# Turning activations by VectorE and a DRAM round trip in place of TensorE transposes, in a two-block fp32 model on one core

## The chip, the core and the metric

The kernel runs on one core of one Trainium2 chip, as one program. The metric is the device time of one execution in microseconds (us), the median of several runs. The engines are named as in the profile: PE (TensorE, matmuls; PEld is its weight load), DVE (VectorE), ACT (ScalarE), POOL (GpSimd), SP (SyncE, which here only issues loads).

## The reference, cut to what matters

A sequence of 256 rows of width 1024 runs, in fp32, through two stacks.

```
first block, 4 layers i:
  h = rms_norm(x);  h = mixer_i(h)          # 0: retention, 1: conformer, 2: short conv, 3: retention
  x = x + rms_norm(h)
  h = relu(rms_norm(x) @ w1)^2 @ w2         # MLP, 1024 -> 4096 -> 1024
  x = x + rms_norm(h)
retention: q,k,v,g = x @ w_in (1024 -> 6144); q,k = rotary(q), rotary(k)
           y = chunked retention(q,k,v), normalised a head; out = (silu(g) * y) @ w_out
short conv: gb,gc,h = x @ w_in;  out = (gb * depthwise_conv3(gc * h)) @ w_out
second block, 2 layers:
  FFN (silu(x@w1) * (x@w3)) @ w2 (1024 -> 2816 -> 1024), layer norm
  token mixing (RWKV-7, GLA, gated delta rule), layer norm
  FFN, layer norm; per-layer-embedding gate, layer norm
```

Every large product has the activations as one operand and a weight matrix streamed from DRAM as the other. Weights are about 470 MB in all.

## The kernel before, in words

**Halves and units.** The 256 rows are two halves, h = 0 and 1, of 128 rows. The weights are a list of *units*, one tile of 128 x 1024 each (the `plan_*` functions). `drive` walks through the list, segment by segment; a segment is a mixer, an MLP, an FFN or the like. At step i half 0 gets unit i and half 1 unit i - lag, where `PACE` gives (lag, ahead, load) for each kind of stage: "1" for the first block, "A" for the FFNs, "M" for token mixing, "B" for its branch products, "P" for the last gate. So at the start of a segment half 0 runs `lag` units alone, and at its end half 1 does, while half 0's normalisation and new left operands are made. A unit is used twice, then released.

**Loading and casting.** `fill` loads up to `load` units ahead (SP, L200) into "raw" buffers, of which there are 3 and 2 more in "1" and "A", and splits up to `ahead` units ahead into a high and a low part in fp32r: `split_unit` copies to `wh` on ACT (L222) and makes `wl` = raw - wh on DVE (L223). There are 4 + 4 slots for these pairs in "1" and "A". A load waits for the cast that frees its raw buffer, a cast for the release of a slot by half 1.

**The product.** `mm3` (matmuls are recorded at L59) multiplies a 128 x 128 block of the left operand, split in the same way (t2h, t2l), in three products into each 512-column group of PSUM: high by high, high by low, low by high. In an MLP or FFN product w1 both groups of 512 go to one bank `mm`, two k-blocks a unit.

**Left operands.** A left operand must have the contracted dimension on partitions, so activations, which come out with rows on partitions, are turned. `tr` (its transposes are recorded at L66) makes four 128 x 128 transposes on PE by the identity into a PSUM bank `tp`; `split` (L348 on ACT, L349 on DVE) reads it and makes t2h and t2l.

**MLP** (`mlp`): the order of units is w1(0), then for each group g of 512 hidden columns w1(g+1), w2(g). After w1(g) ACT makes the relu (L459), DVE its square (L461). For group 0 the turn and split follow w1(1); the others are turned at the second unit of the w2 before them. Eight groups of four + four units.

**FFN** (`ffn`): the same with eleven groups of 256 columns, four units f1 and two f2 a group, silu on ACT (L858), the product on DVE (L860), two transposes a group.

**Retention**: q and k are rotated on DVE (L534 to L540) and turned at once, then copied to SBUF by ACT (rT, L543); 16 units later v is complete and the attention products start. The gated output y2 (L593) is turned and split as soon as each is made, before the product with w_out, whose 16 k-blocks read four such blocks in order. **Short convolution**: gc * h is turned, copied into a window by ACT (L759) and convolved on DVE.

**Buffers.** `B2` gives working tiles from two rings: "s2" of 512 columns, "s1" of up to 264; their sizes are in `RINGS`. In an FFN all group tiles are of the ring "s1".

**Order.** Instructions are issued by each engine in order. `issue_after(ins)` keeps what its block records behind `ins` in that engine's queue.

Of the kernel before, what the change touches and what calls it, by code (L numbers as in the profile page):

```python
# [19 lines left out]

PACE = {"1": (4, 2, 8), "A": (4, 2, 8), "M": (0, 4, 6), "B": (4, 1, 6), "P": (6, 1, 8)}

# [4 lines left out]
RM = (42, 20)  # L27
RINGS = {"1": (30, 6), "A": (20, 6), "M": RM}
SIDE_1 = 1.6
# [21 lines left out]
class Builder:  # L51
    def __init__(s, ctx, tc, io):
# [140 lines left out]
    def load_unit(s, i, early):  # L193
        tag = s.take(s.rawq, early)
        if tag is None:
            return False
        s.slot[i] = [tag, None]
        r = s.r[i] = s.tile_of(tag, F32)
        for dst, src in s.plan[i][1]:
            s.nc.sync.dma_start(dst(r), src)  # L200
        return True

    def split_unit(s, i, early):

        nc = s.nc
        r, n = s.r[i], s.width[i]
        if s.plan[i][0] in EXACT:
            s.w[i] = r
            return True
        tag = s.take(s.whq, early)  # L210
        if tag is None:
            return False
        s.slot[i][1] = tag
        wh, wl = s.tile_of(tag, F32R), s.tile_of(tag, F32R, "l")
        with ExitStack() as st:
            if 2 <= i < 10:

                for ins in s.first_split:
                    st.enter_context(s.tc.issue_after(ins))
            if s.hold is not None and s.hold[0] <= i < s.hold[0] + 4:  # L220
                st.enter_context(s.tc.issue_after(s.hold[1]))
            c = nc.scalar.copy(wh[:, 0:n], r[:, 0:n])  # L222
            nc.vector.tensor_tensor(wl[:, 0:n], r[:, 0:n], wh[:, 0:n].bitcast(F32), op=ALU.subtract)  # L223
# [119 lines left out]
    def split(s, src):  # L343
        nc = s.nc
        n = src.shape[1]
        hh = s.B2((128, n, 128), "t2h", F32R)
        ll = s.B2((128, n, 128), "t2l", F32R)
        a = nc.scalar.copy(hh, src)  # L348
        b = nc.vector.tensor_tensor(ll, src, hh.bitcast(F32), op=ALU.subtract)  # L349
        if s.splits < 2:  # L350
            s.first_split = a.ins, b.ins
        s.splits += 1
        return hh, ll

    def tr(s, src, n=4):
# [3 lines left out]
        return tp  # L359

    def tr_split(s, src):
        return s.split(s.tr(src))

    def linear(s, lhs, KT, name, n=1024, out=None):
# [82 lines left out]
    def mlp(s, h, lhs, rin):  # L447
        nc = s.nc
        out = [s.acc(), s.acc()]
        r = {}  # L450

        def w1(g):
            mm = s.mmb()
            for k in range(0, 8, 2):
                W = yield "w1"
                for kk in range(2):
                    s.mm3(lhs, k + kk, W, [(mm, kk * 512, 512, k + kk == 0, k + kk == 7)])
            a = s.B2(name="relu")
            nc.scalar.activation(a, mm, AF.Relu, scale=rin)  # L459
            a2 = s.B2(name="relu2")  # L460
            nc.vector.tensor_tensor(a2, a, a, op=ALU.mult)  # L461
            r[g] = a2

        yield from w1(0)
        for g in range(8):
            if g < 7:
                yield from w1(g + 1)
            at = nxt if g else [s.tr_split(r.pop(g))]
            for k in range(4):
                W = yield "w2"  # L470
                if g < 7 and k == 1:
                    nxt = [s.tr_split(r.pop(g + 1))]
                s.mm3(at, k, W, [(out[c], c * 512, 512, g == 0 and k == 0, g == 7 and k == 3) for c in range(2)])
        return out
# [49 lines left out]
    def rotary(s, h, ps, rin):  # L524
# [3 lines left out]
        out = []  # L528
        for g in range(2):
# [10 lines left out]
            nc.vector.tensor_tensor(r, a, b, op=ALU.add)  # L540
            tp = s.tr(r.rearrange("p h d -> p (h d)"))
            t = s.B2((128, 4, 128), "rT")
            nc.scalar.copy(t, tp)  # L543
            out.append(t)
        return out

    def retention(s, h, lhs, rin, j):
        nc = s.nc
        sh = s.sh
        q = yield from s.linear(lhs, 8, "ret")  # L550
        qT = s.rotary(h, q, rin)
        k = yield from s.linear(lhs, 8, "ret")
        kT = s.rotary(h, k, rin)
        vs = []
        for c in range(2):
            v = yield from s.linear(lhs, 8, "ret")
            for g in range(2):
# [25 lines left out]
        gn = s.layer_vec(("gn", j), s.io["ret_gn_g"][j])  # L583
        yT = []
        for c in range(2):
            g = yield from s.linear(lhs, 8, "ret")
            for d in range(2):
# [155 lines left out]
    def short_conv(s, h, lhs, rin, j):  # L743
        nc, sh = s.nc, s.sh
        us = []
        for c in range(2):
            ps = yield from s.linear(lhs, 8, "sc1")
            a = s.B2(name="sca")
            nc.scalar.mul(a, ps[0], rin)
            p = s.B2(name="scp")  # L750
            nc.vector.scalar_tensor_tensor(p, ps[1], rin, a, op0=ALU.mult, op1=ALU.mult)
            tp = s.tr(p)
            win = s.pool.tile([128, 4, 130], F32, tag="swin", bufs=4, name="swin")
# [4 lines left out]
            sh["sc", c] = win  # L758
            nc.scalar.copy(win[:, :, 2:130], tp)  # L759
            u = s.B2((128, 4, 128), "scu")  # L760
# [6 lines left out]
            us.append(u)  # L767
        ps = yield from s.linear(lhs, 8, "sc_b")
        hT = []
# [76 lines left out]
    def ffn(s, h, lhs):  # L846
# [4 lines left out]
        def w1(g):  # L851
            mm = s.mmb()
            for k in range(0, 8, 2):
                W = yield "f1"
                for kk in range(2):
                    s.mm3(lhs, k + kk, W, [(mm, kk * 512, 512, k + kk == 0, k + kk == 7)])
# [3 lines left out]
            nc.vector.tensor_tensor(b, a, mm[:, 256:512], op=ALU.mult)  # L860
            r[g] = b

        yield from w1(0)
        for g in range(11):
            if g < 10:
                yield from w1(g + 1)
            at = nxt if g else [s.split(s.tr(r.pop(g), 2)[:, 0:2, :])]
            for k in range(2):
                W = yield "f2"
                if g < 10 and k == 1:  # L870
                    nxt = [s.split(s.tr(r.pop(g + 1), 2)[:, 0:2, :])]
                s.mm3(at, k, W, [(out[c], c * 512, 512, g == 0 and k == 0, g == 10 and k == 1) for c in range(2)])
        return out
# [994 lines left out]
```

## Time and profile before

| | |
|---|---|
| median of 3 runs | 3031.95 us (3026.77 to 3034.68) |
| the profiled execution's own time | 3031.14 us |
| its span, first to last instruction | 3029.3 us |
| granted PE clock | 0.994 |
| busy: PE, DVE, ACT, POOL | 2949.2, 1928.9, 1525.4, 216.6 us |
| transposes on PE of relu, glu, rr, y, scp | 256, 176, 72, 64, 16 |

The profile is of one execution. A row of a group of instructions reads: line of the kernel, engine, operation, output<-inputs, shapes, count | busy us, mean ns of one | idle us of the engine just before them, and what ended it. A row of the timeline reads: start, length, line, operation. A row of the DMA view ends with the KB of one transfer and the median us from issue to landing. A row of waits reads: who waited for whom, us in total, times, longest. Matmuls are pipelined, so their lengths overlap; the distance of their starts tells the pace.

### The profile page before, as it was taken

The page shows a single profiled execution, that of the slowest core. Times are in us where ns is not written, and L with a number is a line of the kernel's source. Part 1 is how long each engine was busy: PE and PEld are TensorE (multiplying, and loading weights), DVE is VectorE, ACT ScalarE, POOL GpSimd, SP SyncE. Part 2 cuts the span into 40 slices and gives each one's busy share as a digit, 9 for nine tenths or more (in the row PEclk, how much of TensorE's full clock was granted, in tenths as well). Part 3 has the DMA queues.
Part 4 walks back from the last instruction along what each step waited for, and adds up shares of the span by engine and source line. Part 5 has one row for each costly group of instructions (what it writes and reads, how often), then busy time and mean ns, then how long its engine had stood idle before and what let it go on. Part 6 is the DMA issues. An engine that isn't in the chain of part 4 may idle for free. (4 is left out here: it accounts for less than half of the span.)

```text
span 3029.3 us, 48491 instructions
## 1 busy us (share of the span) xinstructions
PE 2949.2 (97%) x19034; PEld 2368.4 (78%) x19034; DVE 1928.9 (64%) x3039; ACT 1525.4 (50%) x2348; POOL 216.6 (7%) x352
## 2 busy tenths in 40 slices
PE   8999998999999999999999999999999999999998
PEld 6778877787788778787887777778878778777786
DVE  7565578656755766655557857565665576666656
ACT  4454454545544534544447674444454486643543
POOL 0000025000000000200001000000010000000000
PEclk9999999999999999999999999999999999999999
DMA  7556642566666555665655334366666553334763
GB/s 242 155 180 190 185 152 81 176 187 193 179 191 184 184 167 173 211 187 178 187 173 165 93 92 120 118 207 189 188 203 188 147 147 93 106 112 130 223 188 120
DMA packets 256325, 498.52 MB, mean 165 GB/s; under 512 B 24917, under 2 KB 125473, under 8 KB 256096
## 3 DMA queue, kind: packets, MB, share of 16 engines
q1 hardware_dynamic: 247424, 470.82, 51.1%
q0 software_dynamic: 8096, 22.49, 2.5%
q8 instruction: 150, 2.46, 0.3%
q10 hardware_dynamic: 576, 2.10, 0.2%
q14 instruction: 79, 0.65, 0.1%
HBM read 494.28 MB, written 1.05 MB: 164 GB/s over the span
## 5 line engine op out<-in xcount | busy, mean ns | idle before, releaser
L59 PE MATMUL acc<-wh,t2h 128*128 128x512 f32 (+1 forms) x1512 | 622.0, 413 | 8.6 <-ACT t2h L348 6.1
L223 DVE TENSOR_TENSOR whl<-raw,wh 128x1024 fp32r<-128x1024 f32 x341 | 414.7, 1218 | 293.6 <-ACT wh L222 292.1
L59 PE MATMUL acc<-whl,t2h 128*128 128x512 f32 (+1 forms) x1512 | 594.8, 395 | 0.4 <-DVE whl L223 0.4
L222 ACT CAST wh<-raw 128x1024 fp32r<-128x1024 f32 x341 | 356.7, 1046 | 376.3 <-PE acc L59 252.6
L59 PE MATMUL acc<-wh,t2l 128*128 128x512 f32 (+1 forms) x1512 | 511.5, 395 | 2.1 <-DVE t2l L349 2.0
L223 DVE TENSOR_TENSOR whxl<-raw,whx 128x1024 fp32r<-128x1024 f32 x272 | 330.3, 1216 | 228.6 <-ACT whx L222 228.1
L222 ACT CAST whx<-raw 128x1024 fp32r<-128x1024 f32 x272 | 284.0, 1046 | 272.7 <-PE mm L59 133.9
L59 PE MATMUL acc<-whx,t2h 128*128 128x512 f32 (+1 forms) x856 | 347.9, 407 | 3.0 <-ACT t2h L348 2.9
L59 PEld LDWEIGHTS acc<-wh,t2h 128*128 128x128 f32 x1512 | 286.6, 190 | 78.7 <-ACT t2h L348 14.1
L59 PE MATMUL acc<-whxl,t2h 128*128 128x512 f32 (+1 forms) x856 | 336.3, 393 | 3.3 <-DVE whxl L223 3.3
L59 PEld LDWEIGHTS acc<-wh,t2l 128*128 128x128 f32 x1512 | 284.9, 189 | 67.4 <-DVE t2l L349 5.5
L59 PEld LDWEIGHTS acc<-whl,t2h 128*128 128x128 f32 x1512 | 287.0, 190 | 53.1 <-DVE whl L223 2.0
L59 PE MATMUL mm<-whx,t2h 128*128 128x512 f32 x800 | 313.2, 392 | 2.1 <-ACT whx L222 1.7
L59 PE MATMUL mm<-whx,t2l 128*128 128x512 f32 x800 | 312.1, 390 | 0.8 <-DVE t2l L349 0.8
L59 PE MATMUL mm<-whxl,t2h 128*128 128x512 f32 x800 | 311.8, 390 | 0.8 <-DVE whxl L223 0.8
L59 PE MATMUL acc<-whx,t2l 128*128 128x512 f32 (+1 forms) x856 | 283.6, 392 | 0.5 <-DVE t2l L349 0.5
L223 DVE TENSOR_TENSOR whl<-rawx,wh 128x1024 fp32r<-128x1024 f32 x145 | 177.4, 1225 | 140.8 <-ACT wh L222 140.4
L223 DVE TENSOR_TENSOR whxl<-rawx,whx 128x1024 fp32r<-128x1024 f32 x142 | 173.4, 1222 | 124.9 <-ACT whx L222 124.7
L222 ACT CAST wh<-rawx 128x1024 fp32r<-128x1024 f32 x145 | 152.1, 1050 | 151.9 <-PE acc L59 97.2
L222 ACT CAST whx<-rawx 128x1024 fp32r<-128x1024 f32 x142 | 148.5, 1048 | 140.1 <-PE mm L59 94.6
L59 PEld LDWEIGHTS acc<-whx,t2h 128*128 128x128 f32 x856 | 161.1, 188 | 38.8 <-ACT t2h L348 4.5
L59 PEld LDWEIGHTS acc<-whxl,t2h 128*128 128x128 f32 x856 | 161.5, 189 | 35.9 <-DVE whxl L223 4.8
(613 smaller groups left out, 4143.7 us busy)
## 6 DMA issues: line engine op xcount, KB each, us to landing
raw<-in_mlp_w SPq DMA_DIRECT2D x153, 512.0 KB, 3.7
raw<-in_w_in SPq DMA_DIRECT2D x128, 512.0 KB, 3.7
raw<-in_ffn_w SPq DMA_DIRECT2D x216, 256.0 KB, 3.1
rawx<-in_mlp_w SPq DMA_DIRECT2D x103, 512.0 KB, 3.7
rawx<-in_ffn_w SPq DMA_DIRECT2D x136, 256.0 KB, 3.1
raw<-in_ret_w_in SPq DMA_DIRECT2D x58, 512.0 KB, 4.3
raw<-in_ffn_w SPq DMA_DIRECT2D x53, 512.0 KB, 3.7
rawx<-in_ret_w_in SPq DMA_DIRECT2D x38, 512.0 KB, 4.5
```

Of the source, the lines that this page charges most:

```text
L59: r = m0(out, a, b, **k)
L222: c = nc.scalar.copy(wh[:, 0:n], r[:, 0:n])
L223: nc.vector.tensor_tensor(wl[:, 0:n], r[:, 0:n], wh[:, 0:n].bitcast(F32), op=ALU.subtract)
```

## The change

Activations of MLP, FFN, rotary q and k, gated retention output and short convolution are no longer turned by PE, except for the last group of each MLP and FFN. A new function `tr_dma` turns them in three steps: DVE transposes the 32 x 32 blocks inside the tile (into `tz`); POOL stores the result to a DRAM tile `td` (128 rows of 2 KB, or 1 KB for an FFN's 256 columns); SP loads it back into `ty` in four loads of 32 partitions, each with rows of 512 (256) bytes, so that the blocks land in their places. The loads are put behind the newest weight load in SP's queue. The split (or the copies rT and of the window) reads `ty` in SBUF and is put behind the newest weight cast in ACT's and DVE's order.

The split moves: in MLP and FFN to the third unit of the next w1, in the rotary to the fifth unit of v's second part, for the first two blocks of y2 to the fifth unit of g's second part and for the other two to the fifth unit of the product with w_out, in the short convolution to the fifth unit of the next product. `linear` has a hook `mid` for it, called at k = 4.

Beside this the lag of stages "1" and "A" goes from 4 to 5, "B" from lag 4 and 1 ahead to lag 3 and 2 ahead, and the ring "s1" of stage "A" from 6 to 12 tiles.

```diff
-PACE = {"1": (4, 2, 8), "A": (4, 2, 8), "M": (0, 4, 6), "B": (4, 1, 6), "P": (6, 1, 8)}
+PACE = {"1": (5, 2, 8), "A": (5, 2, 8), "M": (0, 4, 6), "B": (3, 2, 6), "P": (6, 1, 8)}
-RINGS = {"1": (30, 6), "A": (20, 6), "M": RM}
+RINGS = {"1": (30, 6), "A": (20, 12), "M": RM}
...
+        s.dram = pool("dram", 4, space=bass.MemoryType.DRAM)
...
-            s.nc.sync.dma_start(dst(r), src)
+            s.last_load = s.nc.sync.dma_start(dst(r), src).ins
...
+        s.last_cast = c.ins
...
+    def tr_dma(s, src, n):
+        nc = s.nc
+        z = s.B2((128, 4, n, 32), "tz")
+        nc.vector.transpose(z, src.rearrange("p (c a j) -> p a c j", a=4, j=32))
+        d = s.dram.tile([128, 4, n * 32], F32, tag=f"td{n}", bufs=4, name="td")
+        nc.gpsimd.dma_start(d, z.rearrange("p a c j -> p a (c j)"))
+        y = s.B2((128, 4, n, 32), "ty")
+        with s.tc.issue_after(s.last_load):
+            for a in range(4):
+                nc.sync.dma_start(y[32 * a:32 * a + 32].rearrange("i b c j -> i b (c j)"),
+                                  d.rearrange("(b i) a x -> a i b x", b=4)[a])
+        return y.rearrange("p b c j -> p c b j")
+
+    def split_late(s, src):
+        with s.tc.issue_after(s.last_cast):
+            return s.split(src)
...
+            if k == 4 and mid:
+                mid()
...
+                if k == 4 and g:
+                    at[g - 1] = [s.split_late(r.pop(g - 1))]
...
-            r[g] = a2
+            r[g] = s.tr_dma(a2, 4) if g < 7 else a2
...
-            at = nxt if g else [s.tr_split(r.pop(g))]
             for k in range(4):
                 W = yield "w2"
-                if g < 7 and k == 1:
-                    nxt = [s.tr_split(r.pop(g + 1))]
+                if g == 6 and k == 1:
+                    at[7] = [s.tr_split(r.pop(7))]
...
-            tp = s.tr(r.rearrange("p h d -> p (h d)"))
-            t = s.B2((128, 4, 128), "rT")
-            nc.scalar.copy(t, tp)
-            out.append(t)
+            out.append(s.tr_dma(r.rearrange("p h d -> p (h d)"), 4))
...
-                yT.append(s.tr_split(y2))
-        out = yield from s.linear(yT, 16, "ret_o")
+                yy.append(s.tr_dma(y2, 4))
+        out = yield from s.linear(yT, 16, "ret_o", mid=late)
...
-            r[g] = b
+            r[g] = s.tr_dma(b, 2) if g < 10 else b
...
-                if g < 10 and k == 1:
-                    nxt = [s.split(s.tr(r.pop(g + 1), 2)[:, 0:2, :])]
+                if g == 9 and k == 1:
+                    at[10] = [s.split(s.tr(r.pop(10), 2)[:, 0:2, :])]
```

More of the change, by code (lines that the diff above doesn't have):

```diff
@@ L347, in split @@
         ll = s.B2((128, n, 128), "t2l", F32R)
[L348 to L349 removed]
+        cut = (lambda t: t.rearrange("p c (b j) -> p c b j", j=32)) if len(src.shape) == 4 else (lambda t: t)
+        a = nc.scalar.copy(cut(hh), src)
+        b = nc.vector.tensor_tensor(cut(ll), src, cut(hh.bitcast(F32)), op=ALU.subtract)
         if s.splits < 2:
@@ L467, in mlp @@
                 yield from w1(g + 1)
-            at = nxt if g else [s.tr_split(r.pop(g))]
             for k in range(4):
                 W = yield "w2"
-                if g < 7 and k == 1:
-                    nxt = [s.tr_split(r.pop(g + 1))]
-                s.mm3(at, k, W, [(out[c], c * 512, 512, g == 0 and k == 0, g == 7 and k == 3) for c in range(2)])
+                if g == 6 and k == 1:
+                    at[7] = [s.tr_split(r.pop(7))]
+                s.mm3(at[g], k, W, [(out[c], c * 512, 512, g == 0 and k == 0, g == 7 and k == 3) for c in range(2)])
         return out
@@ L540, in rotary, with rotated @@
             nc.vector.tensor_tensor(r, a, b, op=ALU.add)
-            tp = s.tr(r.rearrange("p h d -> p (h d)"))
-            t = s.B2((128, 4, 128), "rT")
-            nc.scalar.copy(t, tp)
-            out.append(t)
+            out.append(s.tr_dma(r.rearrange("p h d -> p (h d)"), 4))
+        return out
+    def rotated(s, ys):
+        out = []
+        with s.tc.issue_after(s.last_cast):
+            for y in ys:
+                t = s.B2((128, 4, 128), "rT")
+                s.nc.scalar.copy(t.rearrange("p c (b j) -> p c b j", j=32), y)
+                out.append(t)
         return out
@@ L550, in retention, with turn @@
         q = yield from s.linear(lhs, 8, "ret")
-        qT = s.rotary(h, q, rin)
+        qy = s.rotary(h, q, rin)
         k = yield from s.linear(lhs, 8, "ret")
-        kT = s.rotary(h, k, rin)
-        vs = []
+        ky = s.rotary(h, k, rin)
+        vs, qT, kT = [], [], []
+        def turn():
+            qT.extend(s.rotated(qy))
+            kT.extend(s.rotated(ky))
         for c in range(2):
-            v = yield from s.linear(lhs, 8, "ret")
+            v = yield from s.linear(lhs, 8, "ret", mid=turn if c else None)
             for g in range(2):
@@ L583, in retention @@
         gn = s.layer_vec(("gn", j), s.io["ret_gn_g"][j])
-        yT = []
+        yT, yy = [], []
+        late = lambda: yT.extend(s.split_late(yy.pop(0)) for _ in range(2))
         for c in range(2):
-            g = yield from s.linear(lhs, 8, "ret")
+            g = yield from s.linear(lhs, 8, "ret", mid=late if c else None)
             for d in range(2):
@@ L745, in short_conv, with taps @@
         us = []
[L746 to L752, printed above, removed]
+        def taps(c, y):
             win = s.pool.tile([128, 4, 130], F32, tag="swin", bufs=4, name="swin")
@@ L758, in short_conv @@
             sh["sc", c] = win
-            nc.scalar.copy(win[:, :, 2:130], tp)
+            with s.tc.issue_after(s.last_cast):
+                nc.scalar.copy(win[:, :, 2:130].rearrange("p c (b j) -> p c b j", j=32), y)
             u = s.B2((128, 4, 128), "scu")
@@ L767, in short_conv @@
             us.append(u)
-        ps = yield from s.linear(lhs, 8, "sc_b")
+        ys = []
+        mid = lambda c: lambda: taps(c, ys[c])
+        for c in range(2):
+            ps = yield from s.linear(lhs, 8, "sc1", mid=mid(0) if c else None)
+            a = s.B2(name="sca")
+            nc.scalar.mul(a, ps[0], rin)
+            p = s.B2(name="scp")
+            nc.vector.scalar_tensor_tensor(p, ps[1], rin, a, op0=ALU.mult, op1=ALU.mult)
+            ys.append(s.tr_dma(p, 4))
+        ps = yield from s.linear(lhs, 8, "sc_b", mid=mid(1))
         hT = []
@@ L854, in w1 @@
                 W = yield "f1"
+                if k == 4 and g:
+                    at[g - 1] = [s.split_late(r.pop(g - 1))]
                 for kk in range(2):
@@ L866, in ffn @@
                 yield from w1(g + 1)
-            at = nxt if g else [s.split(s.tr(r.pop(g), 2)[:, 0:2, :])]
             for k in range(2):
                 W = yield "f2"
-                if g < 10 and k == 1:
-                    nxt = [s.split(s.tr(r.pop(g + 1), 2)[:, 0:2, :])]
-                s.mm3(at, k, W, [(out[c], c * 512, 512, g == 0 and k == 0, g == 10 and k == 1) for c in range(2)])
+                if g == 9 and k == 1:
+                    at[10] = [s.split(s.tr(r.pop(10), 2)[:, 0:2, :])]
+                s.mm3(at[g], k, W, [(out[c], c * 512, 512, g == 0 and k == 0, g == 10 and k == 1) for c in range(2)])
         return out
```

4 lines of the change are left out of this document (3 added, 1 removed).

## The prediction

> **What bounds the kernel now.** I read the page's head first, then a table by stage (one MLP, one FFN), then the chain that ended last, then TensorE's timeline around one transpose.
>
> ```profile
> span 3029.3 us, 48491 instructions
> PE 2949.2 (97%) x19034; PEld 2368.4 (78%) x19034; DVE 1928.9 (64%) x3039; ACT 1525.4 (50%) x2348; POOL 216.6 (7%) x352
> q1 hardware_dynamic: 247424, 470.82, 51.1%
> ```
>
> ```profile
> 845.00:1012.00 167.00, 167.00 (x768) 137.91 (x767) 92.92 (x93) 81.56 (x95) 0.55 (x1) 1.00 0.62 186
> 1425.00:1592.00 167.00, 167.00 (x756) 137.24 (x756) 88.52 (x104) 74.43 (x100) 0.00 (x0) 1.00 0.60 182
> ```
>
> ```profile
> 2304.93 8.16 PE mm L59 x36
> ```
>
> The stage rows (length, then PE, PEld, DVE, ACT and POOL busy, granted clock, DMA share, GB/s) are the inside of an MLP and of an FFN. PE is busy for all 167.00 us at clock 1.00, while DVE has 92.92 and 88.52, ACT less, and the DMA engines 0.62 and 0.60. The chain row gives PE's pace: 36 matmuls in 8.16 us, 0.227 us each. So these stages end when PE's stream ends, and an instruction taken out of that stream is time, if nothing else becomes late. A weight unit is twelve such matmuls (two halves, two column groups, three products): 2.72 us, or 1.36 us for one half alone.
>
> **What is removed.** The price of a transpose is how far it pushes the next matmuls apart.
>
> ```profile
> 604.76 0.39 PE L59 MATMUL mm<-whx,t2l 128*128 128x512 f32 x1
> 604.99 0.60 PE L66 MATMUL tp<-ident,relu 128*128 128x128 f32 x4
> 605.35 0.48 PE L59 MATMUL acc<-wh,t2h 128*128 128x512 f32 x1
> 605.66 0.40 PE L59 MATMUL acc<-whl,t2h 128*128 128x512 f32 x1
> 605.90 0.40 PE L59 MATMUL acc<-wh,t2h 128*128 128x512 f32 x1
> ...
> 1477.58 0.39 PE L59 MATMUL mm<-wh,t2l 128*128 128x512 f32 x1
> 1477.81 0.38 PE L66 MATMUL tp<-ident,glu 128*128 128x128 f32 x2
> 1477.95 0.48 PE L59 MATMUL acc<-whx,t2h 128*128 128x512 f32 x1
> 1478.26 0.39 PE L59 MATMUL acc<-whxl,t2h 128*128 128x512 f32 x1
> 1478.49 0.40 PE L59 MATMUL acc<-whx,t2h 128*128 128x512 f32 x1
> ```
>
> ```profile
> L66 PE MATMUL tp<-ident,relu 128*128 128x128 f32 x256 | 38.3, 272 | 0.0
> ```
>
> From 604.76 to 605.90 lie three matmul steps, which undisturbed take 3 x 0.227 = 0.68 us; they took 1.14. Four transposes cost 0.46 us. The same sum for two (1477.58 to 1478.49) gives 0.91 - 0.68 = 0.23 us. The mean of 272 ns in the last row is a pipelined duration and no price: 528 of them by it would be 144 us, by the starts they are 61.
>
> By the code the change takes away: in the MLPs 4 layers x 2 halves x 7 groups = 56 sets of four (224 of the 256 in the row), 56 x 0.46 = 25.8 us; in the FFNs 4 x 2 x 10 = 80 pairs, 80 x 0.23 = 18.4 us; rotary 2 layers x 2 halves x (q, k) x 2 = 16 sets, gated retention output 16, short convolution 4: 36 x 0.46 = 16.6 us. Together 528 transposes, **60.8 us** of PE. The last group of each MLP and FFN stays on PE.
>
> **What is added, and where it hides.** For each of the 172 blocks: one VectorE transpose, one store by POOL, four loads by SP, each of 32 partitions.
>
> ```profile
> L1107 DVE STREAM_TRANSPOSE invTT<-invT 128x256 f32<-128x256 f32 x20 | 8.7, 435 | 0.1
> L1107 DVE STREAM_TRANSPOSE invTT<-invT 128x128 f32<-128x128 f32 x20 | 6.1, 307 | 0.3
> L147 POOL DMA_DIRECT2D v<-in_norm_g x32 | 18.3, 573 | 58.7 <-DVE t L420 43.3 <-DVE xn L427 14.1 <-DVE xn L404 0.9
> ```
>
> ```profile
> 600.72 0.33 SPq L200 DMA_DIRECT2D rawx<-in_mlp_w  x1
> ```
>
> DVE: 128 more columns cost 0.128 us, so 256 take 0.435 and 512 about 0.69 (estimate from the two rows). 92 x 0.69 + 80 x 0.435 = 98 us, all beside PE: in an MLP group (8 units, 21.8 us) two transposes add 1.4 us to a DVE that is 56% busy. POOL: 172 x 0.573 = 99 us on an engine at 7%. SP: 688 issues x 0.33 = 227 us; SP does nothing but issue loads. Splitting then reads SBUF, not PSUM; I give that no price. None of the three comes near PE's 97%.
>
> DMA: the 172 round trips move 69 MB (92 x 512 KB and 80 x 256 KB, store and load together). Priced by bytes like the queue's row (51.1% for 470.82 MB) that is 7.5 points more over the span; priced by packets, with 128 + 512 rows a block, 110,080 packets and 51.1% for 247,424, it is 22.7. By stage: an MLP group of 21.8 us gets 1.05 MB, 0.16 more by bytes and 0.37 by packets, so 0.78 to 0.99; an FFN group of 16.3 us (6 units) gets 0.52 MB, so 0.71 to 1.09. I take the byte end: the two stage rows move almost the same GB/s at the same share though the FFN's f1 weights come in 1 KB rows and the MLP's in 2 and 4 KB rows, so the share follows bytes.
>
> **The latency, and who waits.** The split of the turned block sits in ACT's queue behind the newest weight cast, and the four loads in SP's behind the newest weight load. If the block is not back, ACT stops and the casts behind it wait, then PE.
>
> ```profile
> L459 ACT ACTIVATE relu<-mm,rin 128x512 f32<-128x512 f32 x64 | 44.2, 690 | 70.1 <-PE mm L59 70.1
> L461 DVE TENSOR_TENSOR relu<-relu 128x512 f32<-128x512 f32 x64 | 44.0, 688 | 33.4 <-ACT relu L459 33.4
> L860 DVE TENSOR_TENSOR glu<-silu,mm 128x256 f32<-128x256 f32 x88 | 36.7, 417 | 30.9 <-ACT silu L858 30.9
> L858 ACT ACTIVATE silu<-mm 128x256 f32<-128x256 f32 x88 | 33.8, 384 | 87.0 <-PE mm L59 87.0
> L349 DVE TENSOR_TENSOR t2l<-tp,t2h 128x512 fp32r<-128x512 f32 x144 | 96.9, 686 | 18.9 <-ACT t2h L348 16.1
> L348 ACT CAST t2h<-tp 128x512 fp32r<-128x512 f32 x144 | 83.1, 586 | 86.2 <-PE tp L66 85.3 <-PE acc L59 0.3
> L349 DVE TENSOR_TENSOR t2l<-tp,t2h 128x256 fp32r<-128x256 f32 x88 | 37.0, 420 | 9.7 <-ACT t2h L348 9.7
> L348 ACT CAST t2h<-tp 128x256 fp32r<-128x256 f32 x88 | 32.6, 371 | 29.6 <-PE acc L59 26.3 <-PE tp L66 3.3
> L59 PE MATMUL acc<-wh,t2h 128*128 128x512 f32 (+1 forms) x1512 | 622.0, 413 | 8.6 <-ACT t2h L348 6.1 <-DVE rb L537 1.7 <-ACT sg L590 0.5
> ```
>
> ```profile
> raw<-in_mlp_w SPq DMA_DIRECT2D x153, 512.0 KB, 3.7
> gv<-in_ret_gn_g POOLq DMA_DIRECT2D x8, 256.0 KB, 5.8
> out<-x ACTq DMA_DIRECT2D x2, 512.0 KB, 2.7
> raw<-in_w_in SPq DMA_DIRECT2D x8, 16.0 KB, 3.1
> ```
>
> No POOL store is in the trace. Its bounds are 2.7 us (the only store, on idle engines at the end) and 5.8 us (the slowest POOL load); I take 4.2, between them, as the store runs among weight loads. A small load lands after 3.1 us, and four issues take 1.3. MLP: 0.69 + 0.69 + 0.69 + 2.7 to 5.8 + 1.3 + 3.1 = 9.2 to 12.3 us to a block that is back, then 1.27 to split. FFN: 0.38 + 0.42 + 0.44 and the same = 8.3 to 11.4 us, then 0.79.
>
> The room in the steady state, from the code: in an MLP six units pass before the split (w2's four, two of the next w1), 16.3 us, in an FFN four, 10.9 us. So MLP blocks are back in time, FFN blocks too but for the last 0.5 us of the bound. Rotary, retention output and short convolution have four units or more: hidden as well.
>
> The first group of each of the eight MLP and FFN runs has less. Half 0 needs it five units later, of which the first runs without half 1: 1.36 + 3 x 2.72 = 9.5 us; half 1 has about 12.2. MLP, block and split: 10.5 to 13.6, late by 1.0 to 4.1 and 0 to 1.4. FFN: 9.1 to 12.2, late by 0 to 2.7 and 0. Four of each: 4 to 33 us, less up to 8 us, since PE already idles there (8.6 us in all before the first matmuls of a split). I take **+10**, ends 0 and +25.
>
> **Slots, queues, lag.** With lag 5 and 2 ahead, eight units are alive in eight slots, where one was spare.
>
> ```profile
> L222 ACT CAST wh<-raw 128x1024 fp32r<-128x1024 f32 x341 | 356.7, 1046 | 376.3 <-PE acc L59 252.6
> L223 DVE TENSOR_TENSOR whl<-raw,wh 128x1024 fp32r<-128x1024 f32 x341 | 414.7, 1218 | 293.6 <-ACT wh L222 292.1
> SPq L200 <- DVE whl L223: 1176.7, 383, 39.5
> L66 PE MATMUL tp<-ident,xn 128*128 128x128 f32 x128 | 20.5, 289 | 13.2 <-DVE xn L404 10.1 <-DVE xn L427 3.1
> ```
>
> A cast already waits for PE to free its slot (252.6 us). It then needs 1.05 + 1.22 = 2.27 us and will have two units, 5.4 us, instead of three: 3.2 us of slack for an ACT that is held. I take **+3**, ends 0 and +20. SP already waits 3.1 us a time for a raw buffer (1176.7 / 383); a load is issued about 3.5 units, 9.5 us, before its cast and lands in 3.7, so 5.8 us of delay by a store's landing and four issues stay hidden. Lag 5 gives 1.36 us more of half 1's matmuls over each layer boundary, where PE idles before the transposes of xn for 13.2 us; **-6**, ends 0 and -17 (a dozen boundaries).
>
> Sum on the profiled execution (span 3029.3 us, its own time 3031.1): 3031.1 - 60.8 + 10 + 3 - 6 = 2977.3; the median of the runs, 3031.95, lies 0.8 above it, so **2978**. The ends of the terms make 2953 to 3017.
>
> **Rivals.**
> *Held ACT, slower.* The split waits in ACT's queue, in the FFNs, where the room is least. Past 10.9 us of room and 3.2 of slack, every further microsecond is lost once for each of 80 blocks. It turns the sign at 10.9 + 3.2 + 60.8/80 = 14.9 us. The upper chain of 11.4 plus one mean load wait of 3.1 on SP is 14.5, so a little more does it: at 15.3 us, 80 x 1.2 = 96 lost, 3031.95 - 60.8 + 96 = 3067. Against it: the chain must be 3.5 us above the bound from rows. Chance 0.10.
>
> *DMA engines become the bound, no change.* At the packet end an FFN group needs 1.09 of its 16.3 us: 1.5 x 40 group times = 60 us, giving back the gain: 3031. For it: rows of 256 bytes, smaller than any bulk load here. Chance 0.06.
>
> *POOL's store is held up by DVE.* A store whose issue stretches over two DVE casts (2 x 1.22 us) makes the chain 2.4 us longer. FFN 13.8 is still inside 14.1, so the steady state holds, but the 16 first blocks lose 2.4 each: 38 us on top, 3016. Against it: POOL's issues took 573 ns on average in a program whose DVE is busy 64%. Chance 0.05. The Trainium skill, "SBUF — State Buffer", section "SBUF: two separate sides", warns that DVE operations that use the port pair they share with GpSimd lock it out of writing descriptors, and gives about 620 ns for such a transfer alone and 3100 beside a DVE copy. By that, the delay would be 2.5 us (an estimate from that page); the 573 ns row does not show it.
>
> *More than forecast.* If boundaries close fully and first groups hide, 3031.95 - 60.8 - 17 = 2954. Inside the main case.
>
> **How the numbers follow.** Main case 0.79, whose own range is 2953 to 3017. Beside it the rivals 0.10, 0.06 and 0.05. The range 2950 to 3017 leaves out the slower and the no-change case, 0.16, and a little of the main one. Measurement of this kernel can tell about 0.3%, 9 us. Faster: 0.79 + 0.05 = 0.84; same 0.06; slower 0.10.
>
> **What would show it.** PE's L66 rows should fall by 528, the tp rows of rr, y and scp vanish, PE's busy time drop by some 60 us at the same share; DVE's L1107-like transposes rise by about 98 us. In the waits, ACT's split should wait on DMA only in the first groups. I am wrong if ACT's split waits on the load of the block all through the FFNs, or if casts and then PE wait on weight loads, or if the DMA share in the FFN window passes 0.9.

## The result, and the profile after

The changed kernel takes **3066.99 us** (median of 4 runs, 3059.68 to 3074.29) where the kernel before, timed beside it, takes 3030.31: a ratio of 1.0118 (95% interval 1.0101 to 1.0135), 36.7 us slower. The forecast was 2978. The profiled execution took 3063.9 us.

The page's head and the granted clock, in which before had PE busy for 2949.2 us and a clock of 0.994:

```profile
span 3062.1 us, 49546 instructions
PE 2917.7 (95%) x18506; PEld 2332.7 (76%) x18506; DVE 2014.2 (66%) x3211; ACT 1517.8 (50%) x2348; POOL 308.8 (10%) x524
```

```profile
core 0: 3062.1 us, clock 0.983
```

PE has 528 instructions fewer, but is busy for only 31.5 us less, since it ran slower (the clock), and it idles longer. The groups say before which instruction (columns as before), and the waits say for whom:

```profile
L59 PE MATMUL acc<-wh,t2h 128*128 128x512 f32 (+1 forms) x1512 | 620.8, 411 | 61.5 <-ACT t2h L351 37.1 <-ACT sg L630 16.2 <-DVE rb L565 6.6
L371 POOL DMA_DIRECT2D td<-tz x172 | 93.8, 545 | 1342.8 <-DVE tz L369 1317.6 <-DVE ang L528 13.4 <-issue 7.8
L369 DVE STREAM_TRANSPOSE tz<-relu 128x512 f32<-128x512 f32 x56 | 39.9, 712 | 1.9
L369 DVE STREAM_TRANSPOSE tz<-glu 128x256 f32<-128x256 f32 x80 | 35.6, 445 | 2.5
```

```profile
ACT t2h L351 <- DMA ty<-td: 84.5, 45, 5.8
PE acc L59 <- ACT t2h L351: 41.4, 28, 6.6
PE acc L59 <- ACT sg L630: 16.2, 7, 7.4
```

```profile
SPq L375 <- DMA td<-tz: 414.7, 146, 10.2
```

The idle time before these matmuls went from 8.6 to 61.5 us; 37.1 of it was ended by a split, 16.2 by a silu. ACT's splits waited 45 times for a turned block, while SP stood 146 times before a block's loads until the store had landed: the blocks are late in some places and not in others. The next rows are from a table by stretches (columns as in the prediction's stage rows); the first is the inside of an FFN:

```profile
1470.00:1590.00 120.00, 120.00 (x526) 97.87 (x525) 69.44 (x87) 54.49 (x73) 7.59 (x14) 1.00 0.72 219
```

There PE is busy for all 120.00 us at full clock with the DMA engines at 0.72: this stretch of the steady state loses nothing. Three places that do lose time follow, each from the timeline (start, length, engine, line; in brackets the idle time before and what ended it).

**The first group of an MLP, half 1.** Rows of ACT, DVE, POOL, SP, ACT and PE, in order of time:

```profile
260.44 0.68 ACT L486 ACTIVATE relu<-mm,rin 128x512 f32<-128x512 f32 x1
262.43 0.71 DVE L369 STREAM_TRANSPOSE tz<-relu 128x512 f32<-128x512 f32 x1
263.44 0.54 POOL L371 DMA_DIRECT2D td<-tz  x1 [4.73 <-DVE tz L369]
265.91 0.85 SPq L201 DMA_DIRECT2D raw<-in_mlp_w  x2
266.85 1.81 SPq L375 DMA_DIRECT2D ty<-td  x4
273.54 0.62 ACT L351 CAST t2h<-ty 128x512 fp32r<-128x512 f32 x1 [4.85 <-DMA ty<-td]
274.21 0.50 PE L59 MATMUL acc<-wh,t2h 128*128 128x512 f32 x1 [2.57 <-ACT t2h L351]
```

From the start of the relu to the start of the split lie 13.1 us; the prediction had 9.2 to 12.3. The store's part is as foreseen (3.4 us to the loads). The loads' part is not: 6.7 us from their first issue, where 1.3 + 3.1 = 4.4 had been put. They stand right behind two weight loads of 512 KB each, and by the first of these stretches the DMA engines are full (1.08):

```profile
268.70:273.50 4.80, 2.94 (x13) 2.09 (x12) 1.23 (x1) 0.00 (x0) 0.00 (x0) 1.00 1.08 303
273.50:279.00 5.50, 4.79 (x14) 3.79 (x15) 3.23 (x4) 2.46 (x4) 0.54 (x1) 0.69 0.37 140
```

ACT does nothing for these 4.80 us, since the split heads its queue.

This block is one of the later ones. Read from the timeline in the same way, the eight first blocks of the MLPs took 9.6 to 14.1 us, 11.4 on average, which is inside what the prediction had. The eight of the FFNs took 10.5 to 14.9 us, 12.3 on average, where it had 8.3 to 11.4. Eleven of the 16 landed within 3.0 to 3.7 us of their first load's issue, for which 4.4 had been put. What made the FFNs' blocks late is the way to that issue: up to 5.7 us from the activation to the store, where 1.2 had been put, and up to 8.3 from the store to the loads, where at most 5.8 had been put.

In an FFN's first group it is also the next weight that is late, since its load was issued late behind SP's wait for the store (ACT, SP, ACT):

```profile
1455.76 1.05 ACT L223 CAST whx<-rawx 128x1024 fp32r<-128x1024 f32 x1 [4.64 <-DMA raw<-in_ffn_w]
1455.97 1.75 SPq L375 DMA_DIRECT2D ty<-td  x4
1459.19 0.71 ACT L351 CAST t2h<-ty 128x256 fp32r<-128x256 f32 x2 [2.38 <-DMA ty<-td]
```

**Retention's product with w_out.** Rows of ACT, then PE, then the clock by stretches:

```profile
193.21 0.62 ACT L351 CAST t2h<-ty 128x512 fp32r<-128x512 f32 x1 [5.28 <-DMA ty<-td]
197.76 0.62 ACT L351 CAST t2h<-ty 128x512 fp32r<-128x512 f32 x1 [3.94 <-DMA ty<-td]
198.29 1.26 ACT L630 ACTIVATE sg<-acc,rin 128x512 f32<-128x512 f32 x2
199.02 0.79 PE L59 MATMUL acc<-wh,t2h 128*128 128x512 f32 x1 [5.87 <-ACT sg L630]
199.61 0.63 PE L59 MATMUL acc<-whl,t2h 128*128 128x512 f32 x1
200.04 0.63 PE L59 MATMUL acc<-wh,t2l 128*128 128x512 f32 x1
```

```profile
186.00:192.00 6.00, 5.82 (x25) 4.68 (x26) 4.53 (x7) 1.93 (x4) 0.54 (x1) 1.00 0.55 169
196.80:203.60 6.80, 4.58 (x11) 3.61 (x12) 4.67 (x7) 1.78 (x3) 0.55 (x2) 0.50 0.34 118
203.60:210.00 6.40, 6.40 (x29) 5.13 (x28) 3.06 (x3) 4.14 (x5) 0.53 (x1) 0.99 0.37 98
```

Half 0's last two blocks of y2 are late. Half 1's silu (sg), which empties the PSUM banks that PE needs next, is queued behind their splits; PE stands for 5.87 us, and from 196.80 to 203.60 the clock is 0.50: the matmuls that then run start 0.43 us apart (199.61, 200.04) in place of 0.227. So a stall is paid again behind it. 3062.1 x (1 - 0.983) = 52 us of the span are clock not granted; before, 3029.3 x (1 - 0.994) = 18. PE's idle time went from 3029.3 - 2949.2 = 80 us to 3062.1 - 2917.7 = 144. The Trainium skill, "TensorE: Matmul & The Clock Gate", section "HAM oscillation — how this bites in real kernels", warns of PE-idle gaps over about 3.4 us. The trace agrees that the clock is halved, and the shortest half-speed stretch in it lasts 3.4 us (275.4 to 278.8); but the gap ahead of that one was 2.57 us (at 274.21, above; mean clock 0.69 from 273.50 to 279.00), so a gap shorter than the page's bound can halve the clock here. Not every gap of this length does (last section).

**POOL's queue in the second block.** Rows of POOL and DVE, then ACT and PE:

```profile
2321.43 0.54 POOL L371 DMA_DIRECT2D td<-tz  x1 [10.04 <-DVE tz L369]
2321.96 0.53 POOL L158 DMA_DIRECT2D rwrow<-in_rw_mu  x1
...
2323.87 0.45 DVE L369 STREAM_TRANSPOSE tz<-glu 128x256 f32<-128x256 f32 x1
...
2332.74 0.56 POOL L1010 DMA_DIRECT2D gab<-in_gdn_a_log  x1
2333.28 0.55 POOL L371 DMA_DIRECT2D td<-tz  x1
```

```profile
2343.17 0.40 ACT L351 CAST t2h<-ty 128x256 fp32r<-128x256 f32 x1 [5.04 <-DMA ty<-td]
2343.62 0.80 PE L59 MATMUL acc<-wh,t2h 128*128 128x512 f32 x1 [6.58 <-ACT t2h L351]
```

Twenty loads of parameters for the coming token mixing are issued between two stores, 11.3 us of them; the next block, turned at 2324.3, waits there for 9.0 us. This is in the third FFN, which is the first of its layer (the expectations below call it the second). Such a burst stands in the last MLP too, but there PE stops for 3.80 us (at 1324.25) for another reason: the burst loads a mask, and a cast of it on DVE stands until it has landed, with a split's low part (t2l) queued behind:

```profile
1323.17 0.43 DVE L995 CAST gmask<-gm 128x512 uint8<-128x512 f32 x1 [4.00 <-DMA gm<-in_c_gmask]
```

Stage lengths put the loss in place. They are measured from ACT's cast of a stage's first weight unit to that of the next stage's, the last gate's to the end of the span, in one profiled execution each, and summed over the stages of a kind (us). The last three columns are runs told below: the pace alone, no wait for the store, and first groups and retention on PE with the old lag.

```
                          before   after   pace alone   no store wait   both, lag 4
retention (2)              409.2   432.2     410.4          398.2          410.3
MLP (4)                    738.9   733.0     739.3          712.5          717.9
FFN (4)                    748.4   770.7     752.8          735.9          733.7
short convolution           98.4    96.3      98.0           96.6           96.6
output projections "B" (2) 169.4   159.3     159.7          159.3          159.4
conformer (1)              139.9   140.5     140.5          140.7          139.0
token mixing (2)           630.3   626.6     623.9          630.3          627.8
gate (2)                    89.1    97.0      86.2           88.4           89.1
```

Token mixing, whose code and pace the change leaves alone, differs by up to 6.4 us between these executions, so a few microseconds in one kind of stage prove little.

### The profile page after: what moved, and what is told of

Same layout as the page of the kernel before. It is cut to its first block, busy times and chain, and to the rows that moved or that the text cites. A ratio compares the mean times of both kernels' runs of the same rounds, so it can differ in the third digit from the quotient of the medians.

```text
span 3062.1 us, 49546 instructions
## 1 busy us (share of the span) xinstructions
PE 2917.7 (95%) x18506; PEld 2332.7 (76%) x18506; DVE 2014.2 (66%) x3211; ACT 1517.8 (50%) x2348; POOL 308.8 (10%) x524
## 5 line engine op out<-in xcount | busy, mean ns | idle before, releaser
L59 PE MATMUL acc<-wh,t2h 128*128 128x512 f32 (+1 forms) x1512 | 620.8, 411 | 61.5 <-ACT t2h L351 37.1
L59 PE MATMUL acc<-wh,t2l 128*128 128x512 f32 (+1 forms) x1512 | 521.0, 398 | 5.2 <-DVE t2l L352 5.2
L224 DVE TENSOR_TENSOR whxl<-raw,whx 128x1024 fp32r<-128x1024 f32 x272 | 329.6, 1214 | 203.9 <-ACT whx L223 189.4
L59 PE MATMUL acc<-whx,t2l 128*128 128x512 f32 (+1 forms) x856 | 292.0, 394 | 5.4 <-DVE t2l L352 5.3
L371 POOL DMA_DIRECT2D td<-tz x172 | 93.8, 545 | 1342.8 <-DVE tz L369 1317.6
```

The costliest lines, as they stand in the source:

```text
L59: r = m0(out, a, b, **k)
L371: nc.gpsimd.dma_start(d, z.rearrange("p a c j -> p a (c j)"))
```

## The experiments

Theory A, formed from these rows and so called in the later expectations: what PE saves is worth what was forecast, but the trip is too long for the room at three places (first groups; retention; the store behind POOL's parameter loads), and the halved clock makes most stalls dearer. Rivals: B, SP's queue, where weight loads stand behind 414.7 us of waiting for stores; C, the steady state of the FFNs; and DMA traffic. The first four expectations still speak of held ACT (ACT stands before a late block), of slots (too few for the weights with the longer lag) and of DMA traffic. Differences are against the kernel before, timed in the same session.

**The pace alone** (the change's `PACE` and `RINGS`, no trip; 3020.91 us, -8.5; ratio 0.9972, 0.9962 to 0.9982).

```diff
-PACE = {"1": (4, 2, 8), "A": (4, 2, 8), "M": (0, 4, 6), "B": (4, 1, 6), "P": (6, 1, 8)}
+PACE = {"1": (5, 2, 8), "A": (5, 2, 8), "M": (0, 4, 6), "B": (3, 2, 6), "P": (6, 1, 8)}
```

> The kernel before with the changed lags (1 and A: 5, B: 3 with 2 ahead) and the changed ring alone; all transposes stay on PE. Held ACT (blocks come back late, ACT stops at their split, PE follows): the lags are not the cause, 3010 to 3030 us. Slots (eight units in eight slots make casts late): the loss is here without any round trip, 3050 us or more. DMA traffic: as held ACT, 3010 to 3030.

The output projections are 9.7 us shorter; retention, MLP and FFN are 1.2, 0.4 and 4.4 longer. The longer lag gains nothing at the boundaries that these stages show. Token mixing is 6.4 us shorter too, no more than such executions differ by; the "B" entry is the one gain that stands out. With 3020.9 us, and not 3050 or more, slots alone are out as the main cause.

**The trip with the old pace** (3030.86 us, +1.4; ratio 1.0004, 0.9995 to 1.0013).

```diff
-PACE = {"1": (5, 2, 8), "A": (5, 2, 8), "M": (0, 4, 6), "B": (3, 2, 6), "P": (6, 1, 8)}
+PACE = {"1": (4, 2, 8), "A": (4, 2, 8), "M": (0, 4, 6), "B": (4, 1, 6), "P": (6, 1, 8)}
```

> The changed kernel with the lags of before (1 and A: 4, B: 4 with 1 ahead), one slot spare again. Held ACT: a shorter lag gives the first blocks less room, 3065 to 3090 us. Slots: the spare slot brings the gain of the removed transposes back, 2980 to 3010. DMA traffic: no change, 3055 to 3075.

None of the three expectations holds: the old pace is 36 us better than the changed kernel, which is less than slots would have given, while held ACT and traffic gave no gain at all. Taking the "B" gain out of the comparison (3030.9 - 9.7 = 3021), lag 5 with its late blocks costs some 46 us. One cause shows in ACT's queue:

```profile
182.54 1.13 ACT L351 CAST t2h<-ty 128x512 fp32r<-128x512 f32 x2
183.57 1.26 ACT L630 ACTIVATE sg<-acc,rin 128x512 f32<-128x512 f32 x2
...
200.98 1.14 ACT L351 CAST t2h<-ty 128x512 fp32r<-128x512 f32 x2
```

With lag 4, half 1's last silu comes before the late splits; with lag 5 it stands behind them (198.29 after 197.76). Retention is 409.9 us here and 432.2 there.

**No trip at all** (2956.80 us, -72.6; ratio 0.9761, 0.9744 to 0.9777) and **no wait for the store** (2966.93 us, -62.5; ratio 0.9791, 0.9777 to 0.9806). In the first the store and the loads are left out and the split reads `z`; in the second all stores and loads stay, and the loads read a constant block.

```diff
+        return z.rearrange("p a c j -> p c a j")
...
-                                  d.rearrange("(b i) a x -> a i b x", b=4)[a])
+                                  s.fixed[n].rearrange("(b i) a x -> a i b x", b=4)[a])
```

> The changed kernel without the store and the loads: the split reads the tile that DVE turned within its 32 x 32 blocks, so the blocks are not put in their places and the output is not the reference's. All of PE's and DVE's work of the change stays. Held ACT: nothing is late any more, 2955 to 2985 us. DMA traffic: the same, 2955 to 2985. Slots or DVE's added transposes: still 3030 or more.

> The changed kernel with all stores and all loads, but the loads read a constant DRAM block that is written once at the start, so SP never waits for a store; the turned activations are that constant and the output is not the reference's. Held ACT and a blocked SP: 2960 to 2995 us, most of the loss gone. DMA traffic: all of it is still there, 3040 us or more.

Against the pace alone, the removed transposes are worth 3020.9 - 2956.8 = 64.1 us, with all that DVE does in their place. Bytes, issues and landings of the trips cost 2966.9 - 2956.8 = 10.1 us, so DMA traffic is out as the main cause. Having the loads wait for the store costs the rest, 3067.0 - 2966.9 = 100 us; this run takes away SP's standing and the late blocks together, so it doesn't tell theory A from B. The idle time before the matmuls that a split releases, without the wait:

```profile
L59 PE MATMUL acc<-wh,t2h 128*128 128x512 f32 (+1 forms) x1512 | 613.4, 406 | 12.3 <-ACT t2h L356 10.2 <-DVE rb L570 1.6 <-ACT sg L635 0.4
```

**Loads issued by POOL** (3189.24 us, +158.0; ratio 1.0515, 1.0496 to 1.0534).

```diff
-        with s.tc.issue_after(s.last_load):
+        with nullcontext():
             for a in range(4):
-                nc.sync.dma_start(y[32 * a:32 * a + 32].rearrange("i b c j -> i b (c j)"),
+                nc.gpsimd.dma_start(y[32 * a:32 * a + 32].rearrange("i b c j -> i b (c j)"),
```

> The changed kernel, but the four loads of a turned block are issued by POOL behind the store, not by SP behind the newest weight load: SP never waits for a store and no weight load is queued behind one. Theory A (the trip itself is too long for the room that the first groups of the eight MLP and FFN runs and the retention's product have, and each such stall is doubled by half-speed clock after it): the trip keeps its store, its landing and its loads, only the wait behind weight loads goes, so a part of the stalls goes: 3040 us, 3015 to 3060. Theory B (SP's queue: weight loads held up behind 414.7 us of waiting for stores, and blocks behind weight loads): all of it goes, 2975 us, 2960 to 2995. Theory C (ACT held through the whole steady state of the FFNs): no change, 3060 to 3070.

All three expectations fell. POOL's waits say why:

```profile
POOL ty L375 <- DMA td<-tz: 214.5, 64, 6.8
...
POOL ty L375 <- ACT t2h L351: 100.5, 26, 5.6
```

POOL is in order too: it now stands at each block's loads until the store has landed, and until ACT has freed the buffer that the loads write, with the next block's store queued behind. The queue that waits was moved to where it hurts more. The run does not decide about SP.

**First groups on PE** (3020.78 us, -10.5; ratio 0.9966, 0.9955 to 0.9978). The edit of the MLP, and the same in the FFN:

```diff
-            r[g] = s.tr_dma(a2, 4) if g < 7 else a2
+            r[g] = s.tr_dma(a2, 4) if 0 < g < 7 else a2
...
+            if g == 0:
+                at[0] = [s.tr_split(r.pop(0))]
```

> The changed kernel with the first group of each half in the eight MLP and FFN runs (16 of 172 blocks) turned on PE again. Theory A: these 16 sets cost PE 5.5 us again and take away the stalls at the first groups; by the lengths of the eight runs (55 us longer in the changed kernel than in the one whose loads don't wait for the store, some 10 us of them at the parameter loads on POOL, which stay) 3030 us, 3015 to 3045. Theory C, or a cause that lies in the weight loads' order all through: 3065 to 3075, the 5.5 us on top.

16 blocks of 172, and 47.2 us of difference to the changed kernel, though PE does 5.5 us more: these blocks cost **53 us**. Theory C is out.

```profile
L59 PE MATMUL acc<-wh,t2h 128*128 128x512 f32 (+1 forms) x1512 | 617.0, 409 | 39.6 <-ACT sg L632 17.5 <-ACT t2h L351 13.8 <-DVE rb L567 6.6
```

```profile
core 0: 3017.3 us, clock 0.989
```

Of the difference, 61.5 - 39.6 = 21.9 us are idle time before these matmuls, and 52 - 33 = 19 us are clock not granted (3017.3 x (1 - 0.989) = 33). Another part lies in the two gates (97.0 us in the changed kernel, 86.3 here), where in the changed kernel DVE worked off a normalisation ahead of a split's low part, for which PE waited 2.65 us (at 2204.37 and 3025.69); why the order differs was not followed.

**Rotary and retention output on PE** (3038.07 us, +6.8; ratio 1.0025, 1.0016 to 1.0035).

```diff
-            out.append(s.tr_dma(r.rearrange("p h d -> p (h d)"), 4))
+            tp = s.tr(r.rearrange("p h d -> p (h d)"))
+            t = s.B2((128, 4, 128), "rT")
+            nc.scalar.copy(t, tp)
+            out.append(t)
...
-                yy.append(s.tr_dma(y2, 4))
+                yT.append(s.tr_split(y2))
```

> The changed kernel with rotary q and k and the gated retention output (32 blocks) turned on PE again. Theory A: the two retention layers, 13.3 and 9.7 us longer than before the change, come back to their old length: 3044 us, 3035 to 3055, though PE does 15 us more. Theory that the retention's blocks are hidden, four units or more ahead, as the prediction had it: 3080 us, 3075 to 3085.

29.9 us better than the change with 14.7 us more on PE: these 32 blocks cost **45 us**. They were not hidden. By the stages, 21.7 us of the 29.9 lie in the retention (432.2 to 410.5); the rest is spread over MLPs and FFNs.

**Both on PE, lag 4** (2982.66 us, -48.6; ratio 0.9840, 0.9823 to 0.9858). Beside the edits of the two runs before:

```diff
-PACE = {"1": (5, 2, 8), "A": (5, 2, 8), "M": (0, 4, 6), "B": (3, 2, 6), "P": (6, 1, 8)}
+PACE = {"1": (4, 2, 8), "A": (4, 2, 8), "M": (0, 4, 6), "B": (3, 2, 6), "P": (6, 1, 8)}
```

> The changed kernel with both of these on PE again (first groups, rotary, retention output), half 1 four units behind half 0 in MLP and FFN as before the change, and the new pace of three units only in the output projections. Theory A: 2990 us, 2975 to 3005: from the 3030.9 of the changed kernel with the old pace, 10 us by the output projections' pace and some 30 us by the stalls of MLP and FFN. If the stalls are not where theory A has them: 3025 to 3040.

Groups, waits and SP's waits of this run:

```profile
L59 PE MATMUL acc<-wh,t2h 128*128 128x512 f32 (+1 forms) x1512 | 613.5, 406 | 9.2 <-ACT t2h L351 6.9 <-DVE rb L567 1.7 <-ACT sg L635 0.5
```

```profile
ACT t2h L351 <- DMA ty<-td: 12.4, 10, 4.3
```

```profile
SPq L375 <- DMA td<-tz: 263.0, 117, 7.4
```

124 blocks still take the trip, SP still stands for 263.0 us before stores that have not landed, and PE idles 9.2 us before splits, as before the change (8.6); the clock is 0.994. So SP's standing costs next to nothing where blocks have room, which speaks against B as the main cause; at the first groups, where a weight came late too, no run tells SP's part from the late block's.

**Both on PE, lag 5** (2993.87 us, -38.8; ratio 0.9875, 0.9858 to 0.9892). The same with the change's `PACE`.

> The kernel with first groups, rotary and retention output on PE, but with half 1 five units behind, as the change has it, in place of four. If the longer lag costs only where a block still comes late: the FFN that has the parameter loads on POOL in it stays long (9.2 us longer than before the change in the kernel with first groups on PE), the rest is as with four units: 3000 us, 2990 to 3008. If the lag costs by itself, in the weights' slots: 3015 us, 3008 to 3025, with ACT's casts waiting on PE in every MLP and FFN. If it costs nothing: 2983 us, as with four.

10 to 11 us more than with lag 4 (by the differences, by the medians); the last MLP (6.3) and the third FFN (7.9), the two stages with POOL's parameter loads, are longer.

**Rotary by the trip** (2985.91 us, -46.8; ratio 0.9846, 0.9831 to 0.9861) and **rotary and the first pair of the retention output by the trip** (2989.24 us, -43.4; ratio 0.9855, 0.9836 to 0.9874), both with lag 4 and first groups on PE. In the first, y2 of both passes is turned by `tr_split`; in the second:

```diff
-                yy.append(s.tr_dma(y2, 4))
+                if c:
+                    yT.append(s.tr_split(y2))
+                else:
+                    yy.append(s.tr_dma(y2, 4))
```

> The kernel with first groups on PE and half 1 four units behind; rotary q and k go through DRAM, the retention output is on PE. If rotary's blocks are hidden, as the prediction had it: 16 sets of 0.46 us less on PE than with all on PE, 2975 us, 2970 to 2979, and the retention's two stretches are 3 to 4 us shorter each. If they come late as the retention output's second pair does: 2983 us or more.

> The kernel with first groups on PE and half 1 four units behind; through DRAM go rotary q and k and the first pair of the retention output (its blocks have a whole product of eight units until they are read), and only the second pair is turned on PE. If the first pair has room enough: 24 sets of 0.46 us less on PE than with all of the retention on PE, 2972 us, 2966 to 2977. If the first pair is late too: 2980 us or more.

In both the second outcome came. The 7.4 and 11.0 us taken off PE brought nothing: retention is 419.2 and 418.4 us, against 410.3 with all on PE. The waits of the first of them show a cast that stood for 15.0 us until a block's load landed, which the run with all of the retention on PE doesn't have:

```profile
ACT wh L223 <- DMA ty<-td: 18.3, 3, 15.0
```

Which order of the queues makes it so was not followed further. The intervals overlap, so by the totals neither run can be told from the one with all of the retention on PE.

**Parameter loads moved**, first to the start of the stage (3071.78 us, +39.1; ratio 1.0127, 1.0105 to 1.0148), then behind the last store (3050.18 us, +21.0; ratio 1.0056, 1.0035 to 1.0078).

```diff
-                if i == max(stop - 36, start) and stop < n and s.kind != "M" and end == stop:
+                if i == start and stop < n and s.kind != "M" and end == stop:
...
+                if i == stop - 4 and stop < n and s.kind != "M" and end == stop:
```

> The changed kernel; only the 20-odd parameter loads that POOL issues for the next token mixing stand at the start of the MLP or FFN before it, ahead of its first store, and not 36 units before its end between two stores. Theory A (they hold up a store for 9 us and PE for 6.7 us, and the clock is halved for 6.8 us after): 3053 us, 3043 to 3059, and the second FFN is 8 to 10 us shorter. If these loads are hidden: 3065 to 3070.

> The changed kernel; the 20-odd parameter loads that POOL issues for the next token mixing stand four units before the end of the MLP or FFN before it, behind the last store of both halves, so that no store waits for them. Theory A: the last MLP and the second FFN, which held them between two stores, are 15 us shorter together: 3052 us, 3043 to 3058. If it was not these loads that made the second FFN 10.3 us longer: 3064 to 3072.

The first missed: in POOL's queue they came after a wait for a normalisation and so once more ahead of a store, the first one of the FFN:

```profile
2250.38 0.56 POOL L158 DMA_DIRECT2D rwrow<-in_rw_mu  x1
...
2263.16 0.54 POOL L371 DMA_DIRECT2D td<-tz  x1
```

The stall moved with them: the last MLP grew from 185.9 to 196.7 us, the third FFN stayed (203.7, 203.9). Behind the last store they hold up no store, and 15.7 us of the change's loss are gone: the last MLP is 5.0 us shorter, the third FFN 8.8.

**The same on top of both on PE**: lag 5, 2985.14 us (-44.1; ratio 0.9848, 0.9834 to 0.9863); lag 4, 2980.71 us (-48.5; ratio 0.9839, 0.9824 to 0.9854).

> First groups, rotary and retention output on PE, half 1 five units behind, and the parameter loads behind the last store. If the 11 us between five units and four are these loads (the last MLP and the second FFN, 6.3 and 7.9 us longer with five): 2982 us, 2976 to 2987. If the longer lag costs by itself: 2990 to 2996 as before they were moved.

> The same with half 1 four units behind. With four units no store was seen to wait for these loads in the second FFN: 2981 us, 2977 to 2985, no measurable change. If they cost there too: 2970 to 2976.

Of the 10 to 11 us between the lags some 6 were these loads; 4.4 us are left, inside the two intervals. The last run has the lowest median of the kernels that leave nothing out, and can't be told from the one at lag 4 with the loads in their old place: both take 1.6% less than the kernel before.

## Why the prediction was wrong, step by step

- **"60.8 us of PE": right.** Measured 64.1, and by stages without the trip: retention 16.7, MLP 26.8, FFN 18.8 less than with the pace alone, predicted 14.7, 25.8, 18.4. The price by distance of starts was the right one.
- **"I take +10, ends 0 and +25" for first groups: the step that failed first.** Measured 53. The waiting was foreseen, its price was not. 21.9 us of idle time before splits lie inside the 4 to 33 us of lateness that the prediction worked out, of which it then took 10. The MLPs' blocks came back as it had them (11.4 us on average, 9.2 to 12.3 put), the FFNs' later (12.3; 8.3 to 11.4 put). And each microsecond late was counted once: the sum has no term for the clock, of which 19 us less were granted than with these blocks on PE, nor for what stands behind the split in ACT's queue. The room was counted up to the matmul that needs the block, while the split holds ACT from the third unit of w1 or f1 on.
- **"Rotary, retention output and short convolution have four units or more: hidden as well": wrong for the first two** (45 us), right for the last (96.3 us from 98.4). The room was counted for the block alone; who stands behind the waiting split on ACT, half 1's silu that frees PE's banks, was not. It is shown for the retention output (5.87 us at 199.02); rotary's part is open.
- **"99 us on an engine at 7%", hidden: wrong by up to 15.7 us**, by 5.3 once the other late blocks are back on PE. A share says nothing of a burst: twenty issues, 11.3 us, stood between two stores. In the last MLP it is the mask's load that DVE waits for. The issue of a store itself was 0.545 us.
- **Lag, "-6": not found.** It closes nothing that the pace alone shows, and with late blocks it costs some 46 us; without late blocks and parameter loads 4.4 us are left, inside the intervals. The 9.7 us of the "B" entry, which were not priced at all, hid some of this.
- **SP, "5.8 us of delay ... stay hidden"**: right in the steady state (263.0 us of standing with 9.2 us of idle PE), wrong at a first group, where a weight came 4.64 us late.
- **Slots, "+3"**: not tried by themselves. With the pace alone, which has both the slots and the lag, retention, MLP and FFN are 6.0 us longer and the gates 2.9 shorter; the two aren't told apart.
- **DMA by bytes: nearly right.** Predicted 0.71 for the FFN, measured 0.72; but the traffic costs 10.1 us where nothing was put.
- **DVE**: transposes of 0.712 and 0.445 us where 0.69 and 0.435 were estimated, hidden as forecast.
- **"If ACT's split waits on the load of the block all through the FFNs"**: by the timeline it waits for 31 of their 80 blocks, but outside the first groups and the parameter loads these are 21 waits of 0.9 us on average, and no PE gap over 0.9 us is behind one. The rival *held ACT* named the mechanism and, by chance, the time (3067), but put it in the 80 blocks of the FFNs' steady state; it is in 48 blocks with less room. The DMA and port rivals fall with 0.72 and with 0.545 us an issue.
- **The ends, 2953 and 3017**: the terms add up to 3031.95 - 60.8 - 17 = 2954 and 3031.95 - 60.8 + 25 + 20 = 3016; the measured 3067 is far outside either way.

The parts close. First groups, rotary and retention output on PE together, at the change's own pace, take 36.7 + 38.8 = 75.5 us off with 20.2 us more on PE: 96 us. Moving the parameter loads then takes off 44.1 - 38.8 = 5.3 more: 101, where all waiting for the store was measured at 100. What stays open is how the 45 us split between rotary and the retention output, and why 8 us of the 29.9 are outside the retention.

## What to carry to other kernels

A turn through DRAM takes work off PE at full price where the block has the room (here 9.6 to 14.9 us at the first groups, where weights are loaded beside it) and nothing that PE needs stands behind its reader; here it paid to keep PE for the first block of every run. Count the room not only for the transfer but for each in-order queue that it passes (POOL's other issues, SP's loads, ACT's casts), and name what stands behind the waiting instruction. Change the lag in a run of its own: here one entry of the pace gained 9.7 us and another lost more.

## What the runs showed of the hardware

- A gap's length alone doesn't decide whether the clock is halved. Gaps of 2.01 us (at 544.20) and 2.57 us (274.21) were followed by 3.4 us at half clock, one of 5.87 us (199.02) by 0.50 from 196.80 to 203.60; but one of 3.09 us, in the run with first groups on PE (at 1991.02), was followed by none. What decides better is how a gap falls. In both traces all half-speed stretches begin on a grid of 3.41 us. In the changed kernel, outside token mixing and the first 23 us, each grid window at full clock in which PE was idle for 0.59 of it or more was followed by half clock, and none with 0.41 or less. The gap of 2.01 us lies in one window (0.59); that of 3.09 us is split between two (0.53 in the fuller one). The limit between is not sharp in the other run (0.45 at 2378.8 was followed by half clock, 0.55 at 190.9 was not), and no run here varies a gap to find it.
- By the mean clock, 52 - 18 = 34 us more than before are clock not granted. With 144 - 80 = 64 us more idle time and 64.1 us of work less, that is about the 32.8 us by which the span grew.
- A store of 128 or 256 KB by POOL lands after 3.5 to 3.7 us; four loads of 32 partitions take 1.75 us to issue on SP, 0.44 each, and land after 2.1 us (rows of 256 bytes) and 2.5 (512) in the median:

```profile
td<-tz POOLq DMA_DIRECT2D x92, 256.0 KB, 3.5
td<-tz POOLq DMA_DIRECT2D x80, 128.0 KB, 3.7
ty<-td SPq DMA_DIRECT2D x368, 64.0 KB, 2.5
ty<-td SPq DMA_DIRECT2D x320, 32.0 KB, 2.1
```

The median hides the worst: at one stage's start a block was back 6.7 us after its first load's issue, behind two weight loads.
